# A planned transformer layer on one core: where a quarter of x is reloaded, and how the planner counts GpSimd DMAs

## The chip, the cores and the metric

The kernel runs on one core of a Trainium2 chip, as one launch. The metric is device time in microseconds (us), the median of three runs of the same program. A further execution was recorded by the hardware profiler; its own time stands in the table below. A core has five engines with an instruction queue each: TensorE (PE in the profile, PEld for its weight loads), VectorE (DVE), ScalarE (ACT), GpSimd (POOL) and SyncE (SP, which here only issues DMAs). Each queue is worked off in order. POOL issues DMAs as well, those that add to what lies in the destination.

## The reference

One layer of a hybrid encoder for 1024 tokens of width 1024, float32. Cut to what matters here:

```python
proj = x @ w_in                       # q, k, v and a forget gate of 8 heads; a second branch; two gates
log_fa = log_sigmoid(f_a + b_f);  F = cumsum(log_fa)
s = q_t . k_s / 8 + F[t] - F[s],  causal;   y_a = softmax(s) @ v        # forgetting attention, 8 heads of 64
y_b = rms_norm(hgrn2(q_b, f_b, i_b)) * norm_g * sigmoid(g_b)             # gated linear recurrence, 4 heads of 128
merged = sigmoid(gate_a) * (y_a @ w_pa) + sigmoid(gate_b) * (y_b @ w_pb)
x = layer_norm(ALPHA * x + merged @ w_o)
x = layer_norm(ALPHA * x + swiglu_ffn(x))
```

## The kernel before, in words

**Precision.** A float32 product is made of three PE matmuls: each operand is split into a rounded high part and the rest (`split`: an ACT copy and a DVE subtraction), and `mm3` multiplies high by high, high by low and low by high.

**Strassen.** Large products run as seven products of quarters instead of eight. x, transposed and split, is held in quarters A11, A12, A21 and A22. `quarter(i, m)` is half i of the channels at half m of the tokens: A21 is `quarter(0, 1)` and A22 is `quarter(1, 1)`; a21 and a22 are the same quarters before the split. Sums of quarters (S1 to S4 in the text below) are made by DVE. S1 takes the place of A21 (`vops["p5"] = A21`, L667), so that A21 must be made again from a21 before its plain use.

**Stages, in the order of the program text.** (1) The products for v and for a value of the second branch, and the forget gates; the sums of the latter go to DRAM as nf_d. (2) `qk_all` makes q and k of the 8 heads in four calls of `qk_strassen`, for pairs of heads in the order 0, 1, 2, 3 (`QORDER`, L36); results go to DRAM as qk_d through `put`. (3) `attention` for four pairs of heads. (4) The second branch, head by head: `hgrn_project` (matmuls bps) and `hgrn`. (5) Gates (ge, gs), the branch projections (pps), the output projection (o), layer norm, the feed-forward part (fa, fb, fc, p), layer norm. Matmuls of (4) and (5) that depend only on x, bps and ge, are filler for PE while (3) and (4) wait on other engines. bps reads both token halves of x, so it needs A21 whole; ge of `gate_part` needs only the first halves.

**box1** (L575) is one 128 x 4 x 1024 tile. First its rows 0 and 1 hold a21 and its rows 2 and 3 hold a22. While the sums are made (L679 to L688) a21 is overwritten by s3 = A11 - a21, which is split for product p7 and stored to DRAM (`sum_d[1]`, L687); then a21 is loaded into the same rows again (L688). In the last call of `qk_strassen`, behind product p5, `split4(A21, a21)` (L764) makes A21 from it.

Later box1 holds the masks of the attention. Head h uses rows r and r+1 with r = 2 for even h and 0 for odd h (L807). Row r gets the head's forget sums, row r+1 the causal constant, both by SP; then POOL issues a DMA that adds the forget sums to row r+1:

```python
sync.dma_start(box1[:, r, :], nf_d[h].partition_broadcast(P))
sync.dma_start(box1[:, r + 1, :], a["causal"])
pool.dma_start(box1[:, r + 1, :], nf_d[h].partition_broadcast(P), accum_op=ALU.add)
```

Each of the three moves 512 KB. A score block s of PSUM is added to its mask by a DVE instruction that also takes the running minimum (`p<-s,box` and `p_w<-s,box` in the profile); ACT exponentiates, POOL scales the rows by the sums' reciprocals (`p<-p,sums`), PE transposes (pt), ACT and DVE split the transposed block (th, tl), and PE multiplies by v (pv). q2, k2 and kl of a head are loaded from qk_d (`qk_load`, L785), k2 and kl into tiles of the tag kb.

**Tiles and slots.** A tile is taken by tag, and each tag has a fixed number of slots (`BUFS`, L399). Tag tt has four slots of 128 x 512; in the stages around the change it holds t2, u2 and the high parts of `put` in each `qk_strassen`, and th and tl in the attention. Tag kb has four; in this stage two are held by the operand S4 of product p3 (L697) and two by the weights of pair 1.

**The order is planned.** The kernel's text doesn't set the order of the instructions. A class `Plan` (L63) records every call with its dependencies. `schedule` (L182) plays the calls through a model with a cost for each: at each step it takes the call that can start first, and by rank among equals. `improve` (L352) then does this `ROUNDS` = 36 more times: each time `latest` computes the latest start of every call from the last result, with a slack that is drawn at random from the seventh round on, and uses it as rank. The order with the earliest modelled end is emitted. In the model SP's transfers run one after the other at 300 bytes per ns (`dma_free`, the time when they are through). A POOL DMA occupies POOL for `SOFT` = 950 ns and lands `LANDS` + bytes / `RATE` = 1050 ns + 524288 / 190 ns later; of POOL's DMAs at most `RING` = 3 are under way, and each lands at least its transfer after the one before.

Nearly every instruction is issued from one line, L384, so the rows of the profile are told apart by the names of their tiles.

Of the kernel before, what the change touches and what calls it, by code (L numbers as in the profile page):

```python
# [62 lines left out]
class Plan:  # L63
# [118 lines left out]
    def schedule(self, slack, wait):  # L182
        calls = self.calls
        tiles = {k: list(v) for k, v in self.tiles.items()}
        users = [[] for _ in calls]
        left = []
        for i, c in enumerate(calls):
            left.append(len(c[4]))
            for m in c[4]:
                users[m].append(i)  # L190
        ready = [0.0] * len(calls)
        self.took, self.after, self.users = [0.0] * len(calls), [], users
        gave = {}
        avail = {q: [] for q in self.queues}
        free = {q: 600.0 for q in self.queues}
        dma_free = 0.0
        ring = [0.0] * RING
        fifo, slots = {}, {}
        for name, i in sorted(self.first.items(), key=lambda kv: (self.turn[kv[1]], kv[1])):
            tag, bufs = self.tiles[name][:2]  # L200
            fifo.setdefault(tag, []).append(name)
            slots.setdefault(tag, [(0.0, "")] * bufs)
        head = dict.fromkeys(fifo, 0)
        for tag in fifo:
            fifo[tag].reverse()
        held = set()
        table = None
        order = {q: [] for q in self.queues}
        for i, c in enumerate(calls):
            if not left[i]:  # L210
                avail[c[0].name].append(i)
        done = 0
        self.times = [0.0] * len(calls)
        while done < len(calls):
            best = None
            for q, av in avail.items():
                for i in av:
                    t = max(free[q], ready[i])
                    ok = True
                    need = {}  # L220
                    for name in calls[i][6]:
                        if name in held:
                            continue
                        tag = self.tiles[name][0]
                        k = need.get(tag, 0)
                        if tag not in LOOSE and name not in self.loose and (len(fifo[tag]) <= k or fifo[tag][-1 - k] != name):
                            ok = False
                            break
                        if len(slots[tag]) <= k:
                            ok = False  # L230
                            break
                        t = max(t, sorted(slots[tag])[k][0] + 60)
                        need[tag] = k + 1
                    if not ok:
                        continue
                    if self.lands[i]:
                        t = max(t, ring[-RING])
                    if q == "ACT":
                        kind = self.kind(calls[i])
                        if kind is not None and kind != table:  # L240
                            t += wait
                    if best is None or (t, self.rank[i]) < best[:2]:
                        best = (t, self.rank[i], i, q)
            if best is None:
                raise RuntimeError("no call can be placed")
            t, _, i, q = best
            c = calls[i]
            avail[q].remove(i)
            d = c[7] * (1 if q in ("PE", "SP") else MARGIN)
            if q == "DVE" and c[8]:  # L250

                d += 0.7 * min(d, max(0.0, free["POOL"] - t))
            if q == "SP":
                start = max(t + 100, dma_free)
                dma_free = start + d
                free[q] = t + 500
                fin = dma_free
            else:
                if q == "ACT":
                    kind = self.kind(c)  # L260
                    if kind is not None and kind != table:
                        table = kind
                        t -= wait
                        d += 1283
                free[q] = t + d
                fin = t + d + self.lands[i]
                if self.lands[i]:
                    fin = max(fin, ring[-1] + self.lands[i] - self.LANDS)
                    ring.append(fin)
            self.times[i] = t  # L270
            self.took[i] = d
            order[q].append((t, i))
            for name in c[6]:
                if name in held:
                    continue
                held.add(name)
                tag = self.tiles[name][0]
                fifo[tag].remove(name)
                s = slots[tag]
                old = min(s)  # L280
                s.remove(old)
                self.after.append((old[1], i))
            for name in c[5]:
                rec = tiles.get(name)
                if rec:
                    rec[2] -= 1
                    rec[3] = max(rec[3], fin + self.LAT[q])
                    if rec[2] == 0:
                        slots[rec[0]].append((rec[3], name))
            for u in users[i]:  # L290
                uq = calls[u][0].name
                lat = self.OWN[q] if uq == q else self.LAT[q]
                if uq == "PE" and q != "PE":
                    lat += slack
                elif uq == "POOL" and q != "POOL":
                    lat += 27
                ready[u] = max(ready[u], fin + lat)
                left[u] -= 1
                if not left[u]:
                    avail[uq].append(u)  # L300
            done += 1
        self.end = max(dma_free + self.LAT["SP"], *free.values())
        return sorted((t, i) for v in order.values() for t, i in v)
# [48 lines left out]
    def improve(self, slack, wait):  # L352


        self.turn = list(range(len(self.calls)))
        best = self.schedule(slack, wait), self.end, self.times
        sound = self.turn, self.rank
        vary = np.random.default_rng(3)
        for n in range(ROUNDS):
            self.rank = self.latest(slack if n < 6 else slack * vary.uniform(0, 3))  # L360
            self.turn = self.rank
            try:
                order = self.schedule(slack, wait)
            except RuntimeError:
                self.turn, self.rank = sound
                order = self.schedule(slack, wait)
            sound = self.turn, self.rank
            if self.end < best[1]:
                best = order, self.end, self.times
        order, self.end, self.times = best  # L370
        return order
# [16 lines left out]
def trunk(ctx: ExitStack, tc, a: dict, out: bass.AP):  # L388
    nc = tc.nc
    plan = Plan(tc)  # L390
    sync, act, dve, pool, pe = (plan.queue(n, e) for n, e in (
        ("SP", nc.sync), ("ACT", nc.scalar), ("DVE", nc.vector), ("POOL", nc.gpsimd), ("PE", nc.tensor)))
# [23 lines left out]
    def half(tag, name, dt=F32):  # L416
        return take(tag, [NB], name, dt)
# [14 lines left out]
    def hs(i):  # L432
        return slice(i * NB, (i + 1) * NB)
# [7 lines left out]
    def split(hi, lo, src):  # L441
        act.copy(hi, src)
        dve.tensor_sub(lo, src, f(hi))
# [64 lines left out]
    def split4(op, raw):  # L508
        for c in range(4):
            split(op[0][c], op[1][c], raw[c])  # L510

    A11, A12, A21, A22 = quarter(0, 0), quarter(1, 0), quarter(0, 1), quarter(1, 1)
# [37 lines left out]
    for k, b, A, p, o in ((0, b11, A11, "p1", vx), (1, b21, A12, "p2", vy)):  # L550
        T = stationary4("v" + p)
        raw = rows(b)
# [24 lines left out]
    a21, a22 = ([box1[:, 2 * i + c // 2, hs(c % 2)] for c in range(4)] for i in range(2))  # L577
# [101 lines left out]
    for c in range(4):  # L679
        s3 = a21[c]  # L680
        dve.tensor_sub(s3, f(A11[0][c]), s3)
        dve.tensor_add(s3, s3, f(A11[1][c]))
        dve.tensor_sub(a22[c], a22[c], s3)
        split(vops["p6"][0][c], vops["p6"][1][c], a22[c])
        split(vops["p7"][0][c], vops["p7"][1][c], s3)
        sync.dma_start(sum_d[0, c], a22[c])
        sync.dma_start(sum_d[1, c], s3)  # L687
        sync.dma_start(s3, a["xT"][c][:, hs(1)])  # L688
    product("p6", T2, vx, True)
    for t in range(4):  # L690
        dve.tensor_add(vbm[:, t, :], vx[t], p1v[t])
# [39 lines left out]
    def qk_strassen(p, wtags, btags, last=False):  # L731
# [29 lines left out]
        dve.tensor_sub(b12, b12, b11)  # L761
        mul("p5", b12, oc, True)
        if last:
            split4(A21, a21)  # L764
        t2 = take("tt", [4, P], f"wqk{p}_t2")
        dve.tensor_sub(t2, b22, b12)
        mul("p2", b21, ob, True)
# [111 lines left out]
    raw = half("gt", "once_r")  # L879
# [371 lines left out]
    for i, src in enumerate((ya_d, yb_d)):  # L1251
        yh, yl = [], []
        for c in range(4):
            if i == 0:
                raw, rest = (take(f"wr{a_}", [S], f"yr{a_}{c}") for a_ in range(2))
# [547 lines left out]
```

## Time and profile before

| | us |
|---|---|
| median of 3 runs | 1436.33 (1436.11 to 1436.84) |
| the profiled execution, its own time | 1436.61 |
| span of its instructions | 1434.8 |
| mean granted TensorE clock | 0.996 |
| PE busy | 1419.1 (99% of the span) |
| DVE busy | 1104.8 (77%) |
| ACT busy | 657.0 (46%) |
| POOL busy | 90.9 (6%) |

The span begins at 0 with the first instruction, and all times in the rows are counted from there. A row of a timeline has start, duration, engine, line, operation, output<-inputs, shapes and a count; in square brackets stands the idle time of the engine before it and who ended it. In the view of waits a row says who waited for whom, the total in us, how often, and the longest. In the table of windows each row is a stretch of time with, for PE, PEld, DVE, ACT and POOL, the busy time and in brackets the number of instructions, then the granted clock of PE as a share of full speed, the busy share of the 16 DMA engines, and GB/s. Rows of DMA issues end with the median us from issue to landing. Matmul ends are modelled and overlap, so the rate of matmuls is read from the distance of their starts.

### The profile page before, as it was taken

Reading aid. Unit: us, or ns where it says so; the run is one execution under the profiler, and the core shown is the slowest. Engines: PE = TensorE matmul, PEld = TensorE weight load, DVE = VectorE, ACT = ScalarE, POOL = GpSimd, SP = SyncE. Lnnn points to the kernel's source line nnn. Section 1 sums busy time; section 2 is a strip of 40 time slices with the busy share of each in tenths; the row PEclk is TensorE's granted clock in tenths of the full one; section 3 lists DMA queues with packets and bytes.
Section 4 is the critical chain, followed back from the end, with each engine's and each line's share of the span. In section 5 each row is a group of like instructions: output and inputs, shape, how many; then the busy total and the mean of one; then the engine's idle time right before and its main releaser. Section 6 shows DMA issues by size and latency. Waiting matters only on the chain.

```text
span 1434.8 us, 18979 instructions
## 1 busy us (share of the span) xinstructions
PE 1419.1 (99%) x6722; PEld 1180.1 (82%) x6722; DVE 1104.8 (77%) x1912; ACT 657.0 (46%) x1164; POOL 90.9 (6%) x108
## 2 busy tenths in 40 slices
PE   9999989999999999999999999999999999999997
PEld 7788878888888888888888888888888888888886
DVE  7995868899888978546757997666766776789597
ACT  5534668986778632244511543333333334444330
POOL 0000233420001000000001000000000000000001
PEclk9999999999999999999999999999999999999999
DMA  7456999811112677457500233333333325878632
GB/s 269 168 181 234 290 270 280 236 60 45 45 59 75 217 229 231 151 199 271 176 1 20 84 103 119 101 104 110 110 111 110 100 93 200 326 257 271 215 130 88
DMA packets 92158, 227.39 MB, mean 158 GB/s; under 512 B 10512, under 2 KB 11792, under 8 KB 92064
## 3 DMA queue, kind: packets, MB, share of 16 engines
q1 hardware_dynamic: 90912, 221.99, 47.1%
q0 software_dynamic: 1152, 4.19, 1.5%
q8 instruction: 53, 0.87, 0.3%
q14 instruction: 41, 0.34, 0.1%
HBM read 167.62 MB, written 58.52 MB: 158 GB/s over the span
## 4 chain that ended last, share of the span: by engine, by line
PE 95%; DVE 3%; DMA 1%; ACT 1%; issue 0%; POOL 0%; SPq 0%; DVEq 0%; POOLq 0%
PE p L384 15%; PE fb L384 11%; PE bps L384 9%; PE gs L384 8%; PE fc L384 8%; PE fa L384 8%; PE o L384 6%; PE pps L384 6%; PE vx L384 4%; PE qk_s L384 2%; PE s L384 2%; PE vy L384 2%; PE pv L384 2%; PE ge L384 2%; PE qk_h L384 2%; PE pt L384 2%
## 5 line engine op out<-in xcount | busy, mean ns | idle before, releaser
L384 PE MATMUL p<-dp 128*128 128x512 f32 (+1 forms) x957 | 210.0, 382 | 0.0
L384 PEld LDWEIGHTS p<-dp 128*128 128x128 f32 x957 | 175.3, 188 | 34.8
L384 PE MATMUL fc<-xs,Tp 128*128 128x512 f32 x528 | 127.3, 389 | 0.8 <-ACT Tp L384 0.8
L384 PE MATMUL fb<-xs,Tp 128*128 128x512 f32 x528 | 127.2, 389 | 0.0
L384 PEld LDWEIGHTS fc<-xs,Tp 128*128 128x128 f32 x528 | 99.1, 188 | 21.8 <-ACT Tp L384 1.2
L384 PEld LDWEIGHTS fb<-xs,Tp 128*128 128x128 f32 x528 | 99.1, 188 | 20.5
L384 PE MATMUL fa<-x,Tp 128*128 128x512 f32 x480 | 115.6, 389 | 0.0
L384 ACT CAST Tp<-t 128x512 fp32r<-128x512 f32 x88 | 54.1, 620 | 118.5 <-PE fc L384 64.8
L384 DVE TENSOR_TENSOR Tp<-t,Tp 128x512 fp32r<-128x512 f32 x88 | 60.7, 691 | 61.2 <-ACT Tp L384 60.6
L384 PEld LDWEIGHTS fa<-x,Tp 128*128 128x128 f32 x480 | 90.1, 188 | 18.7
L384 PE MATMUL bps<-xh,wb_h 128*128 128x512 f32 x192 | 76.9, 401 | 0.1
L384 PE MATMUL bps<-xl,wb_h 128*128 128x512 f32 x192 | 76.6, 400 | 0.0
L384 PE MATMUL bps<-xh,wb_l 128*128 128x512 f32 x192 | 76.6, 402 | 0.0
L384 POOL TENSOR_TENSOR norm<-norm,few 128x1 f32<-128x1 f32 x16 | 15.4, 963 | 910.7 <-DVE norm L384 910.7
L384 ACT CAST dp<-dap 128x1024 fp32r<-128x1024 f32 (+1 forms) x42 | 41.1, 979 | 54.2 <-PE p L384 32.3
L384 DVE TENSOR_TENSOR dp<-dap,dp 128x1024 fp32r<-128x1024 f32 (+1 forms) x42 | 47.5, 1132 | 22.2 <-ACT dp L384 22.2
L384 DVE TENSOR_TENSOR tl<-pt,th 128x512 fp32r<-128x512 f32 (+1 forms) x96 | 51.3, 551 | 9.5 <-ACT th L384 5.3
L384 PE MATMUL fb<-x,Tp 128*128 128x512 f32 x240 | 57.6, 389 | 0.0
L384 ACT CAST Tp<-wg_r 128x512 fp32r<-128x512 f32 x40 | 24.9, 623 | 62.0 <-PE fb L384 30.0
L384 PEld LDWEIGHTS fb<-x,Tp 128*128 128x128 f32 x240 | 45.0, 188 | 9.4
L384 ACT CAST th<-pt 128x512 fp32r<-128x512 f32 (+1 forms) x96 | 45.2, 478 | 15.5 <-PE pt L384 8.9
L384 DVE TENSOR_TENSOR u<-fb,p 128x512 f32<-128x512 f32 x40 | 27.7, 692 | 29.4 <-PE fb L384 29.4
(705 smaller groups left out, 3456.5 us busy)
## 6 DMA issues: line engine op xcount, KB each, us to landing
dbp<-in_w_fo SPq DMA_DIRECT2D x45, 512.0 KB, 4.7
dap<-a_d SPq DMA_DIRECT2D x35, 512.0 KB, 4.6
wg_r<-in_w_ff SPq DMA_DIRECT2D x22, 512.0 KB, 3.7
wu_r<-in_w_ff SPq DMA_DIRECT2D x22, 512.0 KB, 3.7
a_d<-ar SPq DMA_DIRECT2D x42, 256.0 KB, 2.7
a_d<-as SPq DMA_DIRECT2D x33, 256.0 KB, 2.3
qk_d<-qk SPq DMA_DIRECT2D x32, 256.0 KB, 4.4
wg_r<-in_w_g SPq DMA_DIRECT2D x16, 512.0 KB, 4.6
```

Source lines behind the costliest of these rows:

```text
L384: getattr(q.engine, method)(*args, **kw)
```

## The change

Three edits. (1) The reload of a21 into box1 behind the stores of the sums is gone. Instead, in the last `qk_strassen`, each of its four parts is loaded into a tile of tag tt, and split into A21 from there. The same bytes are loaded, and the same splits are made. (2) In `schedule` the landing of a POOL DMA is put off by the time for which SP's transfers are still under way when it is issued, and half of its transfer time is charged to `dma_free`, so that later SP transfers are put off as well. (3) The random generator of `improve` starts from seed 1 instead of 3.

```diff
@@ Plan.schedule
                 free[q] = t + d
                 fin = t + d + self.lands[i]
                 if self.lands[i]:
+                    fin += max(0.0, dma_free - t - d)
+                    dma_free = max(dma_free, t + d) + 0.5 * (self.lands[i] - self.LANDS)
                     fin = max(fin, ring[-1] + self.lands[i] - self.LANDS)
                     ring.append(fin)
@@ Plan.improve
-        vary = np.random.default_rng(3)
+        vary = np.random.default_rng(1)
@@ trunk, the sums of the quarters
         sync.dma_start(sum_d[0, c], a22[c])
         sync.dma_start(sum_d[1, c], s3)
-        sync.dma_start(s3, a["xT"][c][:, hs(1)])
@@ qk_strassen
         mul("p5", b12, oc, True)
         if last:
-            split4(A21, a21)
+            for c in range(4):
+                raw = half("tt", f"a21_{c}")
+                sync.dma_start(raw, a["xT"][c][:, hs(1)])
+                split(A21[0][c], A21[1][c], raw)
         t2 = take("tt", [4, P], f"wqk{p}_t2")
```

## The prediction

> **What bounds the kernel now.** First the page, for the room that TensorE (PE) leaves at all.
>
> ```profile
> span 1434.8 us, 18979 instructions
> ...
> PE 1419.1 (99%) x6722; PEld 1180.1 (82%) x6722; DVE 1104.8 (77%) x1912; ACT 657.0 (46%) x1164; POOL 90.9 (6%) x108
> ```
>
> PE is idle for 1434.8 - 1419.1 = 15.7 us. No other order can win more than that and what a slow clock costs. Next the view of waits, of PE over the whole span; it names all of PE's waits:
>
> ```profile
> PE s L384 <- DVE soft L384: 5.1, 1, 5.1
> PE vy L384 <- DVE few L384: 1.2, 1, 1.2
> PE fc L384 <- ACT Tp L384: 0.8, 1, 0.8
> PE s L384 <- DMA kl<-qk_d: 0.6, 1, 0.6
> PE pt L384 <- DVE tl L384: 0.2, 1, 0.2
> ```
>
> They sum to 7.9 us. The other 7.8 us is nearly all tail: in the chain of waits the last run of matmuls ends at 1384.96 + 42.38 = 1427.34, 7.5 us before the span does.
>
> ```profile
> 1384.96 42.38 PE p L384 x218
> ```
>
> The change edits nothing there. So one wait is worth looking at, the 5.1 us before a score matmul (s). PE's timeline around it:
>
> ```profile
> 178.54 0.65 PE L384 MATMUL s<-kl,q 128*128 128x128 f32 x3 [0.65 <-DMA kl<-qk_d]
> ...
> 180.28 0.39 PE L384 MATMUL bps<-xh,wb_l 128*128 128x512 f32 x1
> 180.51 0.39 PE L384 MATMUL bps<-xh,wb_h 128*128 128x512 f32 x1
> 186.01 0.69 PE L384 MATMUL s<-k,q 128*128 128x384 f32 x1 [5.12 <-DVE soft L384]
> ...
> 188.10 0.63 PE L384 MATMUL bps<-xh,wb_l 128*128 128x512 f32 x1
> 188.53 0.63 PE L384 MATMUL pv<-th,vhl 128*128 128x512 f32 x1
> ```
>
> A 512-column matmul follows the last one after 0.23 us ahead of the gap and after 0.43 us behind it. The windows of 2 us show why; the column behind POOL's is the granted clock:
>
> ```profile
> 184.00:186.00 2.00, 0.00 (x0) 0.00 (x0) 0.34 (x3) 0.01 (x1) 0.06 (x1) 0.50 1.02 258
> 186.00:188.00 2.00, 1.99 (x5) 1.79 (x6) 1.49 (x8) 2.00 (x7) 0.81 (x1) 0.50 1.04 372
> 188.00:190.00 2.00, 2.00 (x6) 1.52 (x6) 1.21 (x4) 0.39 (x2) 0.00 (x0) 0.50 1.02 408
> 190.00:192.00 2.00, 2.00 (x12) 1.72 (x11) 1.53 (x4) 1.97 (x3) 1.39 (x3) 0.80 1.07 261
> ```
>
> All engines stand still, and the clock is halved inside the gap. From 186 on it costs 2 x 0.50 + 2 x 0.50 + 2 x 0.20 = 2.4 us more. Only the DMA engines (the share behind the clock) are full. What did DVE wait for? DVE's, POOL's and SP's timelines:
>
> ```profile
> 165.23 0.69 DVE L384 TENSOR_TENSOR xl<-box,xh 128x512 fp32r<-128x512 f32 x1
> ...
> 185.66 0.29 DVE L384 CUSTOM_DVE_ANT_0 p<-s,box 128x128 f32<-128x128 f32 x1 [8.56 <-DMA box<-nf_d]
> ...
> 199.58 0.29 DVE L384 CUSTOM_DVE_ANT_0 p<-s,box 128x128 f32<-128x128 f32 x1 [0.36 <-PE pt L384]
> ```
>
> ```profile
> 98.28 1.06 POOL L384 DMA_DIRECT2D box<-nf_d  x1 [97.85 <-DVE vbm L384]
> ...
> 170.07 4.65 POOL L384 TENSOR_SCALAR p<-p,sums 128x640 f32<-128x640 f32 x4 [4.89 <-DVE sums L384]
> 174.67 0.89 POOL L384 DMA_DIRECT2D box<-nf_d  x1
> 185.94 0.87 POOL L384 DMA_DIRECT2D box<-nf_d  x1 [10.38 <-DMA box<-in_causal]
> ```
>
> ```profile
> 56.75 2.18 SPq L384 DMA_DIRECT2D box<-in_xT  x4
> ...
> 162.37 0.32 SPq L384 DMA_DIRECT2D box<-nf_d  x1
> ...
> 166.43 0.54 SPq L384 DMA_DIRECT2D box<-in_causal  x1
> ...
> 168.21 1.33 SPq L384 DMA_DIRECT2D kl<-qk_d  x2
> ...
> 173.92 0.33 SPq L384 DMA_DIRECT2D box<-in_causal  x1
> ```
>
> Head 0's mask is issued by POOL at 98.28, long before its use. Head 1's lies in box1 rows 0 and 1, which hold a21, reloaded at 56.75 and not read out before the last xl<-box at 165.23 + 0.69 = 165.9. So its causal part is issued at 166.43, and POOL, which first ends four scalings, adds to it at 174.67. That lands 10.83 us later by the chain of waits, at 185.5, and DVE goes on at 185.66:
>
> ```profile
> 174.67 10.83 DMA box<-nf_d
> ```
>
> **The change part by part.** *Removed:* the four reloads of 56.75. They cost SP 2.18 us; no PE wait in the list above is near 57 us, so their going wins nothing. Rows 0 and 1 are then free from about 57 us on, since the reload too had to wait until they were read out; nf_d, which the mask needs, exists by 98.28, when head 0's POOL DMA reads it. *Moved:* head 1's two SP loads, of 0.32 + 0.54 us, and its POOL DMA of 0.89 us go from 162-175 to about 98-115. SP passes them ahead of the weights of pairs 2 and 3 and of everything at 120-162, POOL ahead of all its scalings. That is 1.5 MB. Is there room?
>
> ```profile
> 104.00:110.00 6.00, 6.00 (x28) 4.97 (x27) 2.98 (x7) 2.51 (x5) 0.00 (x0) 1.00 1.00 332
> 110.00:116.00 6.00, 6.00 (x28) 4.98 (x27) 3.16 (x5) 1.57 (x3) 0.00 (x0) 1.00 0.19 73
> ...
> 146.00:152.00 6.00, 6.00 (x29) 4.95 (x28) 5.18 (x9) 3.23 (x7) 0.00 (x0) 1.00 0.77 301
> ```
>
> At 332 GB/s 1.5 MB are 4.7 us, and 110-116 alone has 0.81 x 6 = 4.9 us of idle DMA. The mask is there some 50 us before head 1 needs it, and costs nothing. *Added:* four 256 KB loads of a21 (again about 2.2 us of SP) in the last strassen, 5 to 25 us ahead of splits that end at 165.9: an estimate from the landings below, 140-158. At 301 GB/s 1 MB is 3.5 us of full DMA; 146-152 has 0.23 x 6 = 1.4 us free, so some 2 us of backlog may be left at 158. Nothing waits for PE there yet. Against it stand the 1.5 MB that no longer go out at 162-185: at the 258 GB/s of the gap 6 us less ahead of all that follows. ACT and DVE split the same four halves, from another tile, at the same price. *A new wait:* each raw tile needs one of the four tt slots, which the puts of q and k, t2, u2 and the attention's th and tl turn over. SP issues in order, so a raw load that waits for a slot holds back the qk_d stores and the q, k and kl loads of heads 0 and 1, and PE waits for those (0.65 us at 178.54). Below: nothing (PE has no wait there to win back), when the planner puts the loads where slots are free. Above: one landing of a qk_d store (10.4 us, next fence) for each round. I take nothing, and price the upper end as a rival.
>
> So **what goes** is 5.12 + 2.4 = 7.5 us. **What is late next?** First kl, then head 2's mask; the DMA issues of 164-172, 172-176 and 176-186, with median us to landing at the end:
>
> ```profile
> qk_d<-qk SPq DMA_DIRECT2D x2, 256.0 KB, 10.4
> ...
> kl<-qk_d SPq DMA_DIRECT2D x2, 256.0 KB, 9.4
> ...
> box<-in_causal SPq DMA_DIRECT2D x1, 512.0 KB, 11.7
> ...
> box<-nf_d POOLq DMA_DIRECT2D x1, 512.0 KB, 8.4
> ```
>
> Head 1's kl needs a kb slot and so can't be issued before 168.21; it lands at about 178.5. DVE could then start at about 178.9, not 185.66; PE has work until 180.9. The 5.12 us go, the 0.65 us I keep. Head 2's causal part (173.92 + 11.7 = 185.6) and POOL's add (185.94 + 8.4 = 194.3) are used at 199.58, which comes at about 192 without the gap. Unmoved, the mask would be 2.2 us late; with 6 us less ahead of it, it is in time by some 4 us.
>
> **The planner's two edits** reorder everything. The new model delays a GpSimd DMA by SP's backlog and charges SP half its transfer. By the code the old one let it land 1.05 + 2.76 = 3.8 us after issue; the rows say 10.83 and 8.4, so later masks are planned nearer the truth. Seed 1 draws other slacks. Neither adds an instruction. The size of what an order leaves in small waits is that of the short ones above, 0.2 to 1.2 us; I take no change, and 2 us either way.
>
> **Sum**, against the profiled execution (1436.61 us, 1.8 outside its span): 1436.6 - 7.5 = 1429.1. The median of the three runs is 0.3 lower, which gives 1428.8. I predict 1429.0. Removing all five PE waits would be 1436.3 - 7.9 - 2.4 = 1426.0, the floor.
>
> **The rivals.** (A) *Head 2's mask, or another, takes the gap's place.* DMA is full behind the gap (1.02 to 1.07 in 184-192, above), and the gap gave later transfers 7.5 us of lead. Unmoved, head 2's costs 2.2 us: 1431.2; with a halved clock behind it 2.2 + 2.4: 1433.6; two such, 1438, which is its far end. For it: masks land 8 to 12 us after issue. Against it: the bytes taken out, and a plan that knows of them. [...]
>
> (B) *Nothing comes of it:* the planner, free to choose, still places head 1's mask or something else that scores need (q and k come late through the same full DMA) so that the 5.1 us stay: 1435 to 1438.
>
> (C) *Slower: the tt slots.* Two raw loads wait a round each, SP stands still behind them, and A21 is whole late. Before, it is whole at 165.9 and the filler matmuls (bps) that read it start at 171.93:
>
> ```profile
> 171.93 0.39 PE L384 MATMUL bps<-xh,wb_h 128*128 128x512 f32 x1
> ```
>
> That is 6.0 us of cover. One round (10.4) and a landing (5.4, the median of box<-in_xT among the DMA issues, below) make 15.8 us; 9.8 of it is PE idle, and 2.4 of clock make 12.2. Less the 7.5 won: 1436.3 + 4.7 = 1441. It decides from 6.0 + 5.1 = 11.1 us of lateness on, and counts as slower from 14. For it: four more tiles of some 7 us each in four slots while two strassens overlap. Against it: the planner counts slots, and puts of pairs 2 and 3 are not urgent.
>
> ```profile
> box<-in_xT SPq DMA_DIRECT2D x12, 256.0 KB, 5.4
> ```
>
> **How the numbers follow.** The forecast (1426 to 1431.2) has 0.54; A 0.20, B 0.08, C 0.18. This kernel's measurement tells 0.2%, 2.9 us, from no change: faster is below 1433.5, slower above 1439.2. Faster: the forecast and 0.12 of A, 0.66. Same: 0.08 of A and B, 0.16. Slower: C, 0.18. The range reaches from 0.5 above the floor to the end of B, 1426.5 to 1438.0, and leaves out C and a little at the floor. The forecast's own range is 1426.5 to 1431.2.
>
> **What would show it.** POOL issues two adds to box near 98-105, the next not before 175. DVE's 8.56 us wait for box and PE's 5.12 us are gone, and the clock is 1.00 in all windows from 160 to 200. box<-in_xT appears near 140-158, into other tiles. A shows as POOL or DVE waiting for box with PE idle near 185-200; C as an SP wait ahead of the raw loads and PE idle at 160-175. A new PE wait over 3 us elsewhere would mean that the reordering, not the mask, decides.

## The result, and the profile after

| | us |
|---|---|
| kernel after, median of 6 runs | 1428.11 (1427.25 to 1428.72) |
| kernel before, median of 6 runs beside it | 1436.22 (1435.34 to 1437.18) |
| ratio after / before | 0.9943, 95% interval 0.9930 to 0.9956 |
| profiled execution of after, its own time | 1427.78 (before 1436.61) |

The change makes the kernel 8.1 us faster; the profiled executions differ by 8.8 us. First the page of after, its span and busy times:

```profile
span 1425.8 us, 18971 instructions
...
PE 1415.6 (99%) x6722; PEld 1178.1 (83%) x6722; DVE 1104.2 (77%) x1912; ACT 659.1 (46%) x1166; POOL 89.2 (6%) x108
```

The span is 9.0 us shorter. PE's idle time is now 1425.8 - 1415.6 = 10.2 us instead of 15.7: 5.5 us less. The other 3.5 us are busy time that went; 2.4 of them are the halved clock behind the old gap, and 1.1 I can't tie to a place. Next the whole list of PE's waits in after:

```profile
PE vy L386 <- DVE few L386: 1.2, 1, 1.2
PE fc L386 <- ACT Tp L386: 0.8, 1, 0.8
PE s L386 <- DVE soft L386: 0.3, 1, 0.3
PE pt L386 <- DVE tl L386: 0.3, 1, 0.3
```

They sum to 2.6 us against 7.9. The 5.1 us before a score matmul are gone, and so are the 0.6 us for kl. The windows of 2 us where before had stood still, columns as above:

```profile
184.00:186.00 2.00, 1.73 (x9) 1.17 (x8) 1.11 (x5) 1.99 (x6) 0.77 (x2) 1.00 1.03 411
186.00:188.00 2.00, 2.00 (x12) 1.59 (x12) 1.84 (x10) 2.00 (x6) 2.00 (x4) 1.00 1.02 400
188.00:190.00 2.00, 2.00 (x11) 1.73 (x10) 0.87 (x2) 2.00 (x4) 0.46 (x2) 1.00 1.10 352
```

PE works, the clock is 1.00, and the DMA engines are as full as they were. Three timelines of after show the moved work: POOL, then SP, then DVE.

```profile
99.41 1.98 POOL L386 DMA_DIRECT2D box<-nf_d  x2 [98.98 <-DVE wqk_t L386]
...
187.25 0.85 POOL L386 DMA_DIRECT2D box<-nf_d  x1
```

```profile
58.13 0.36 SPq L386 DMA_DIRECT2D box<-in_causal  x1
...
75.78 0.33 SPq L386 DMA_DIRECT2D box<-in_causal  x1
...
100.15 0.86 SPq L386 DMA_DIRECT2D box<-nf_d  x2
...
152.62 0.39 SPq L386 DMA_DIRECT2D a<-in_xT  x1
...
170.06 0.34 SPq L386 DMA_DIRECT2D a<-in_xT  x1
...
177.59 0.34 SPq L386 DMA_DIRECT2D box<-in_causal  x1
```

```profile
174.35 0.29 DVE L386 CUSTOM_DVE_ANT_0 p<-s,box 128x128 f32<-128x128 f32 x1 [0.35 <-POOL p L386]
...
176.57 1.22 DVE L386 TENSOR_TENSOR xl<-a,xh 128x512 fp32r<-128x512 f32 x1 [1.10 <-ACT xh L386]
...
199.45 0.29 DVE L386 CUSTOM_DVE_ANT_0 p<-s,box 128x128 f32<-128x128 f32 x1
```

The masks of heads 0 and 1 are both begun at 58 to 76 and both added to at 99.41. Head 1's is first read at 174.35 instead of 185.66, and nobody waited for it. In the same stretch a21 comes in raw, the fourth part issued as late as 170.06 and split until 176.57 + 1.22 = 177.8, after the first bps of PE's timeline:

```profile
170.12 0.39 PE L386 MATMUL bps<-xh,wb_h 128*128 128x512 f32 x1
```

Head 2's mask, issued from 177.59 on and added to at 187.25, is read at 199.45.

### The profile page after: what moved, and what is told of

It reads as the page before. It is cut to its first block, busy times and chain, and to the rows that moved or that the text cites. A ratio compares the mean times of both kernels' runs of the same rounds, so it can differ in the third digit from the quotient of the medians.

```text
span 1425.8 us, 18971 instructions
## 1 busy us (share of the span) xinstructions
PE 1415.6 (99%) x6722; PEld 1178.1 (83%) x6722; DVE 1104.2 (77%) x1912; ACT 659.1 (46%) x1166; POOL 89.2 (6%) x108
## 4 chain that ended last, share of the span: by engine, by line
PE 77%; DVE 2%; ACT 0%; issue 0%; DVEq 0%
PE p L386 15%; PE fb L386 11%; PE gs L386 8%; PE fc L386 8%; PE fa L386 8%; PE bps L386 7%; PE o L386 6%; PE pps L386 6%; PE ge L386 2%; PE lp L386 2%; PE op L386 1%; PE pv L386 1%; PE pt L386 1%; DVE xs L386 0%; PE x1t L386 0%; PE up L386 0%
```

## The experiments

**The theories.** The first is that of the prediction: head 1's mask came late, everything waited for it, and after is faster because that mask is there early. Its rival: each of the three edits makes the planner draw another order of the whole kernel, and what decides is which transfer that order leaves late in the stretch where DMA is full. The two part where the mask alone is moved in an order held fixed, and where the edits are taken singly or with other seeds. Each kernel computes the whole layer. The kernel before ran beside them on the same chips, with medians of 1435.86, 1436.92 and 1436.13 us for the first four, the next four and the last four runs. Those of before moved by up to 1.1 us from one set to the next, so that differences of 1 us between runs of different sets tell nothing. Letters in the expectations name theories, M the first of the two above; rivals A to C are those of the prediction. Below, "the reload" is the new place of a21's reload, "the cost" the new cost of a POOL DMA.

**1. Head 1's mask back where it was, in after's order.** One line in the function that emits the calls gives three DMAs other places in the queues and leaves every other instruction in its order:

```diff
-        order = self.improve(slack, wait)
+        at = dict(zip(range(self.mask[1], self.mask[1] + 3), (161900.0, 165000.0, 174020.0)))
+        order = sorted((at.get(i, t), i) for t, i in self.improve(slack, wait))
```

(`mask[h]` is the number of the first of the three mask calls of head h, noted where they are recorded; times in ns.)

> The changed kernel with its own order held instruction by instruction on all engines; only head 1's three mask DMAs are moved back to about where the kernel before had them (its two SP loads among the k loads near 162-166, the POOL add just ahead of the first read, near 175). Theory M (the time is lost where a mask lands after its planned first read): add issued near 175, landing 8 to 11 us later, DVE waits 9 to 12 us from 174.4 on, PE idles 5 to 8 us with the clock halved behind it: 1435 to 1440. Rival R (the new order and seed did it, the mask's place is worth little because the new order has filler there): at most 1431. Rival D (what helped is the 1.5 MB taken out of the full DMA stretch): some of the loss without a DVE wait for box, 1430 to 1433.

Measured: 1439.54 us (1439.01 to 1443.32, 5 runs), ratio to before 1.0034 [1.0020, 1.0049]. POOL's timeline, DVE's, then PE's waits and its windows:

```profile
175.46 0.88 POOL L386 DMA_DIRECT2D box<-nf_d  x1
```

```profile
185.41 0.29 DVE L386 CUSTOM_DVE_ANT_0 p<-s,box 128x128 f32<-128x128 f32 x1 [11.05 <-DMA box<-nf_d]
```

```profile
PE pt L386 <- DVE tl L386: 8.6, 2, 8.4
```

```profile
182.00:184.00 2.00, 0.00 (x0) 0.00 (x0) 0.00 (x0) 0.00 (x0) 0.00 (x0) 0.71 1.00 260
184.00:186.00 2.00, 0.00 (x0) 0.00 (x0) 0.59 (x3) 0.00 (x0) 0.00 (x0) 0.50 1.12 299
186.00:188.00 2.00, 1.64 (x6) 1.54 (x7) 1.38 (x4) 1.36 (x4) 1.41 (x1) 0.50 0.99 328
```

The gap is back, with the halved clock, and DVE stands 11.05 us for the mask. Three DMAs moved, and all of the gain is lost and 3 us more: 11.4 us over after. The early mask is needed for after's time. Rival D, by which only the bytes taken out of the full stretch had helped, expected no such wait for box; those bytes came back as well, so what they cost by themselves is not told apart. In that order PE reaches the mask sooner than before did (DVE's wait begins at 174.36 instead of 177.10), so that the gap is 8.4 us and not 5.1.

**2. The same three; the second is planned 2.5 us and the third, the add, 6 us earlier than in 1** (161900, 162500, 168000).

> As late_add_held, but the three mask DMAs are moved back less: SP loads near 162, POOL add between its scalings near 168 to 172. [...] R: 1428 to 1429, no PE wait.

Measured: 1437.19 us (1435.25 to 1440.42, 10 runs), 1.0011 [1.0002, 1.0021]. POOL's timeline and PE's waits:

```profile
172.27 0.91 POOL L386 DMA_DIRECT2D box<-nf_d  x1 [5.58 <-DMA box<-in_causal]
```

```profile
PE pt L386 <- DVE tl L386: 6.2, 2, 5.9
```

POOL waited for the causal part, so the add went out only 3.2 us earlier than in 1, and the gap shrank by 2.5. It was meant to leave a gap of a few us and so to show the clock behind a short one; it left 5.9, and the clock fell as in 1, to 0.50 in 180 to 186. What it does show is the slope: 3.2 us of the add's start are 2.5 us of gap and 2.4 us of time. The intervals of the two ratios touch, so it rests on the rows more than on the times.

**3. The new cost alone** (before with the cost, seed 3).

```diff
                 if self.lands[i]:
+                    fin += max(0.0, dma_free - t - d)
+                    dma_free = max(dma_free, t + d) + 0.5 * (self.lands[i] - self.LANDS)
```

> The kernel before with the planner's new cost of POOL DMAs alone (a21 still reloaded early into box1, seed 3). Here the planner puts head 1's first read some 15 us after the POOL add (by its own times 193 and 178), where the kernel before had 5. M: the mask is late but nobody waits for it, PE has other matmuls there: 1430.5 to 1433.5, no DVE wait for box over 2 us. Rival E (only the early mask, so only the reload, removes the gap): 1435 to 1438, the PE wait of about 5 us still there.

Measured: 1441.20 us (1439.12 to 1447.02, 5 runs), 1.0044 [1.0026, 1.0063]. DVE's timeline and PE's waits:

```profile
191.03 0.69 DVE L386 TENSOR_TENSOR tl<-pt,th 128x512 fp32r<-128x512 f32 x1 [10.39 <-DMA qk_d<-qk]
```

```profile
PE pt L386 <- DVE tl L386: 9.8, 2, 9.2
```

A miss. DVE waits for no mask here, though head 1's add goes out only at 178.25, and yet it is the slowest of all. DVE wants a tt slot for a tl, and the slot is held by a part of q or k that `put` is still storing. Such stores take 11.3 us to land in this stretch (the median of qk_d<-qk among the DMA issues of 164 to 186). That nobody waits for the mask is not enough.

**4. The reload alone** (before with the reload, seed 3).

```diff
-        sync.dma_start(s3, a["xT"][c][:, hs(1)])
...
-            split4(A21, a21)
+            for c in range(4):
+                raw = half("tt", f"a21_{c}")
+                sync.dma_start(raw, a["xT"][c][:, hs(1)])
+                split(A21[0][c], A21[1][c], raw)
```

> The kernel before with the new place of the reload alone (old cost of POOL DMAs, seed 3). Head 1's mask is early. Head 2's add is planned at 185 and its first read at 190, with a landing 3.8 us after issue; measured landings are 8 to 11 us. M: the gap at head 1 goes and a shorter one opens at head 2: DVE waits 3 to 6 us, PE idles 0 to 3 us: 1430 to 1434. Rival E (the reload is the whole gain): 1428 to 1429.5, no new wait for box.

Measured: 1435.65 us (1431.93 to 1437.41, 10 runs), 0.9996 [0.9986, 1.0005]: no gain. POOL's timeline, DVE's, PE's waits, and the windows:

```profile
185.03 0.89 POOL L384 DMA_DIRECT2D box<-nf_d  x1
```

```profile
195.06 0.29 DVE L384 CUSTOM_DVE_ANT_0 p<-s,box 128x128 f32<-128x128 f32 x1 [5.31 <-DMA box<-nf_d]
```

```profile
PE pv L384 <- DVE tl L384: 4.1, 1, 4.1
```

```profile
194.00:196.00 2.00, 0.39 (x2) 0.39 (x3) 0.57 (x4) 0.00 (x0) 0.28 (x1) 0.92 1.05 246
196.00:198.00 2.00, 2.00 (x8) 1.71 (x7) 1.57 (x6) 1.63 (x5) 0.84 (x1) 0.50 1.02 266
198.00:200.00 2.00, 2.00 (x10) 1.53 (x9) 0.82 (x4) 1.19 (x4) 0.00 (x0) 0.73 1.04 195
```

This is rival A of the prediction in full: head 1's mask is early, so head 2's is asked for at 195.06 - 5.31 = 189.75, 9.8 us sooner than before's 199.58, and it is the one that is late. The gap is 4.1 us, and the halved clock behind it costs 0.16 + 1.00 + 0.54 = 1.7 us more: 5.8 of the 7.5 us won are given back at the next mask, and the rest goes into small waits.

**5. Reload and cost together, seed 3 kept.**

> Both mechanisms of the change, seed 3 as before: the reload's new place and the new cost of POOL DMAs. Theory M2 (each of the two edits alone leaves a wait: the reload alone one at head 2's mask, the cost alone one elsewhere in the full DMA stretch; together they leave none, and the seed is incidental): 1427.5 to 1431, no PE wait over 2 us between 140 and 300. Rival S (the seed was picked for the chip; other seeds leave gaps as before): 1433 to 1441.

Measured: 1437.82 us (1436.12 to 1440.18, 10 runs), 1.0010 [1.0001, 1.0019]. ACT's timeline and PE's:

```profile
187.06 0.58 ACT L386 CAST th<-pt 128x512 fp32r<-128x512 f32 x1 [4.62 <-DMA qk_d<-qk]
```

```profile
188.42 1.12 PE L386 MATMUL pt<-ident,p 128*128 128x128 f32 x4 [4.18 <-DVE tl L386]
```

Both masks are in time here, and the place of the late transfer is taken by a store that holds a tt slot. So with seed 3 the two real edits do not give the gain either; after differs from this kernel by one digit, the seed, and by 9.7 us.

**6, 7, 8. The other three combinations**: the cost with seed 1, the reload with seed 1, and seed 1 alone.

```diff
-        vary = np.random.default_rng(3)
+        vary = np.random.default_rng(1)
```

> The change without the reload's new place: new cost of POOL DMAs, seed 1, head 1's mask still in rows that are free only near 166. M2: its planned first read is some 14 us after the add, so no wait for box, but three mask DMAs (1.5 MB) stay in the full stretch 160-190 and a store or load there lands later than planned: a PE wait of 2 to 10 us as with the cost alone: 1434 to 1442. Rival P (honest costs are enough, the model_only loss was a matter of its seed): 1429 to 1434.

> The change without the new cost of POOL DMAs: reload in its new place, seed 1. Head 2's add is planned at 184 and its first read at 190, as in reload_only. M2: a wait for box at head 2 of 3 to 6 us on DVE, 2 to 5 us on PE: 1431 to 1436. Rival S (the seed is what counts): about 1428.

> The kernel before with seed 1 alone. Head 1's add is planned at 173 and its first read at 177. M2: DVE waits 5 to 9 us for box at head 1, as before: 1434 to 1438. Rival S: about 1428 to 1431.

Measured: 1434.47 us (1432.95 to 1435.70, 10 runs), 0.9983 [0.9974, 0.9993]; 1439.78 (1436.11 to 1441.81, 10 runs), 1.0021 [1.0011, 1.0030]; 1437.47 (1434.14 to 1439.59, 10 runs), 1.0003 [0.9992, 1.0014]. PE's waits of the first of them, the cost with seed 1:

```profile
PE pt L386 <- DVE tl L386: 2.5, 4, 1.2
PE gs L386 <- DVE gu L386: 1.4, 2, 1.0
```

the two longest of the reload with seed 1:

```profile
PE pt L384 <- POOL p_w L384: 2.6, 1, 2.6
PE qk_h L384 <- ACT qk_p L384: 1.9, 1, 1.9
```

and of seed 1 alone, DVE's and PE's:

```profile
DVE p L384 <- DMA box<-nf_d: 4.5, 1, 4.5
```

```profile
PE s L384 <- DVE soft L384: 4.0, 1, 4.0
```

Seed 1 alone waits for head 1's mask as seed 3 did. The first loses its time in many waits of 1 us. Of the second's two longest waits, the one of 2.6 us, near 308, is behind POOL's scalings, with neither mask nor store in it, and a halved clock follows. The one of 1.9 us, near 116, is behind a store again: ACT, which makes qk_p, had just stood 5.2 us for a store of v (v_d<-v). All its PE waits come to 10.4 us against 2.6 in after, and the halved clock adds 1.7: 9.5 of the 11.3 us between the two profiled executions. All eight combinations:

| | seed 3 | seed 1 |
|---|---|---|
| neither | 1436.2 (before) | 1437.5 |
| the reload | 1435.7 | 1439.8 |
| the cost | 1441.2 | 1434.5 |
| reload and cost | 1437.8 | 1428.1 (after) |

No edit has a price of its own. The reload moves the time by -0.5, +2.3, -3.4 or -6.4 us, depending on what else is set, the cost by between +5.0 and -11.7, the seed by between +4.1 and -9.7.

**9. Head 2's mask a little earlier, in the order of 4.** Its causal part goes ahead of one kl load on SP, its add ahead of one scaling on POOL; all else is held.

```diff
-        order = self.improve(slack, wait)
+        at = {self.mask[2] + 1: 174600.0, self.mask[2] + 2: 183500.0}
+        order = sorted((at.get(i, t), i) for t, i in self.improve(slack, wait))
```

> reload_only with its own order held; only head 2's causal load moves up by one kl load in SP's queue and its POOL add up by one scaling (512 wide) in POOL's, as early as head 0's last read of that row allows. Theory W (reload_only lost its gain to head 2's mask, and only to that): the add is issued some 2 us earlier, DVE's wait for box falls from 5.3 to about 3 us, PE's gap from 4.1 to 1 to 2.5 us, and the halved clock may go: 1430.5 to 1434 against 1435.65. Theory S (the loss is spread over the new order, one wait replaces the next): 1435 to 1436.

Measured: 1434.44 us (1431.99 to 1437.86, 11 runs), 0.9988 [0.9979, 0.9997], against 0.9996 [0.9986, 1.0005] of 4. POOL's timeline and PE's waits:

```profile
183.82 0.91 POOL L384 DMA_DIRECT2D box<-nf_d  x1 [2.21 <-DVE sums L384]
```

```profile
PE pv L384 <- DVE tl L384: 2.8, 1, 2.8
```

The add could go only 1.2 us earlier, since POOL still stood behind scalings that waited for sums. The gap fell from 4.1 to 2.8, by 1.3: in this order head 2's mask does end the wait, us for us. The median fell by 1.2, but the two intervals overlap, so the runs alone would not show it.

**10, 11, 12. Further seeds:** all edits with seeds 4 and 10, and the kernel before with seed 6.

> The changed kernel with seed 4 in place of 1. Theory S (in the stretch where the DMA engines are full, each order has some transfer that lands later than planned; the seed decides whether someone waits for it): anywhere from 1428 to 1441, with a PE wait of 2 to 9 us between 170 and 200 when it is above 1432; no wait for head 1's mask in any case. Theory M2 (both edits together are enough): 1428 to 1431.

> The changed kernel with seed 10, whose order has nearly the modelled end of seed 1's (0.4 us later by the planner's own model). S: 1428 to 1441, the modelled end tells little. M2: 1428 to 1430.

> The kernel before with seed 6 in place of 3; head 1's mask free only near 166, its add planned at 173, its first read at 176. W and S alike: DVE waits 5 to 10 us for head 1's mask, as before and with seed 1: 1434 to 1440. If it came out below 1431, the reload's place would not be needed at all.

Measured: 1433.14 us (1430.85 to 1435.12, 8 runs), 0.9977 [0.9966, 0.9987]; 1431.67 (1431.06 to 1433.19, 6 runs), 0.9971 [0.9959, 0.9984]; 1440.07 (1438.66 to 1441.44, 8 runs), 1.0025 [1.0015, 1.0036]. PE's longest wait in each of the three:

```profile
PE pt L386 <- DVE tl L386: 2.8, 3, 2.1
```

```profile
PE pt L386 <- DVE tl L386: 1.7, 1, 1.7
```

```profile
PE s L384 <- DVE soft L384: 6.2, 1, 6.2
```

In the first two, DVE waited with a tl for a store (qk_d<-qk) that held a tt slot, for 4.0 us (in two waits) and 2.3 us. In the third it waited for head 1's mask, for 6.6 us at the longest.

**What follows.** Sort the orders by what is in them. The old text, with seeds 3, 1 and 6, gives 1436.2, 1437.5 and 1440.1: mean 1437.9, and in each PE stands still for 4.0 to 6.2 us over head 1's mask. The new text, with seeds 1, 3, 4 and 10, gives 1428.1, 1437.8, 1433.1 and 1431.7: mean 1432.7, and none waits for that mask; three of the four wait for a store in its stead. So the change is worth about 5 us over these few orders. The spread is 3.9 us within the old text and 9.7 within the new, and of the 35 ways to pick three of these seven times, 3 pick times as slow as the old text's or slower: that the new text is faster in the mean is likely, not shown. The reload alone and the cost alone, with two seeds each, have means of 1437.7 and 1437.8, no better than the old text. After is the best order of those tried, by 3.6 us over the next. Why seed 1's order leaves no slot behind a late store stays open: the stores' median landing does not tell it (7.3 us in after, 6.6 in 5, 8.2 and 9.3 with seeds 10 and 4).

## Why the prediction came right, and which step of it failed

- *The gap and the clock behind it, 7.5 us:* right, and shown by 1. Together with the 0.65 us for kl, which I kept and which went, that is 8.1 to 8.2 us, the measured difference of the medians. The sum was short by that one term.
- *Head 1's mask DMAs at 98 to 115 cost nothing:* right. The adds went out at 99.41 and landed 10.9 us later, some 60 us ahead of their use.
- *Head 2's mask in time by some 4 us:* right for after. With 8.9 us, the median landing of the adds in 177 to 202, it is there at 196.2 and read at 199.45, 3.3 us to spare. But it is no property of the change: in 4 it was 5.3 us late, and rival A happened there.
- *Nothing for the tt slots, with 6.0 us of cover and a bound of 11.1 us (rival C):* the outcome was right and the reason wrong. A21 was whole at 177.8, 11.9 us later than before's 165.9, beyond the bound, and PE did not wait: bps begins 7.7 us before A21 is whole, so its first matmuls don't read all of it. I had taken the start of the first bps for the moment at which A21 is needed. The slots did cost, but in other orders and elsewhere: not a raw load waiting for a store, but DVE and ACT waiting for a th or tl behind one (3, 5, 10, 11).
- *The planner's two edits: "I take no change, and 2 us either way":* **this step failed.** I sized it by the short waits that were left in one order, 0.2 to 1.2 us. The same text with four seeds spans 1428.1 to 1437.8 us, and the cost with seed 3 alone makes 1441.2. The forecast holds only because after's order is the one in which nothing follows the gap. That is luck of the seed: nothing in the prediction says why seed 1 should draw it. By its own steps run 5, with the same two edits of substance, should have been as fast, and it was 9.7 us slower. (The 3.8 us that it gives for the old model's landing begin where POOL is through; counted from the start of the issue, as the rows count, they are 4.8.)
- *"A new PE wait over 3 us elsewhere would mean that the reordering, not the mask, decides":* after has none; 3 and 5 have one of 9.2 and of 4.2 us. Both theories hold a part: the mask had to go early, and the order had to leave nothing else late.
- *Rival A's two prices for 2.2 us of wait, 1431.2 with the clock left alone and 1433.6 with it halved:* no row of before tells which of them holds, and the runs show both kinds. The gap of 1.74 us in run 11 was followed by 1.7 us of lost clock, so that it cost 3.4 us; one of 1.92 us in run 7 lost no clock.

## What to carry to other kernels

Where the DMA engines are full (a share of about 1.0 from 160 to 200 here), a late transfer that is moved away makes the next one due sooner (head 2's mask by 9.8 us in 4): look up every transfer and every slot held by a store in that stretch, and count the gain only down to the next of them. In a planned kernel an edit and the order that is drawn for it can't be told apart by one run; run the edit with several seeds, and test its mechanism with the order held and only the suspected instructions moved. An engine's first use of a stage is not the first use of the tile that you worry about: find the row that reads the tile.

## What the runs showed of the hardware

**Behind a PE gap of 1.74 us the clock was halved, and only after PE was back at work; behind one of 1.92 us it was not.** The gap of 1.74 us is that of seed 10 (run 11). PE's timeline, then windows of 1 us:

```profile
186.16 0.44 PE L386 MATMUL pt<-ident,p 128*128 128x128 f32 x2 [1.74 <-DVE tl L386]
```

```profile
186.00:187.00 1.00, 0.84 (x6) 0.67 (x6) 1.00 (x6) 0.00 (x0) 0.34 (x1) 1.00 1.05 424
187.00:188.00 1.00, 1.00 (x5) 0.91 (x5) 1.00 (x5) 0.58 (x1) 0.00 (x0) 0.69 0.99 391
188.00:189.00 1.00, 1.00 (x4) 0.90 (x4) 0.88 (x4) 1.00 (x4) 0.01 (x1) 0.50 1.08 420
189.00:190.00 1.00, 1.00 (x4) 0.74 (x3) 0.00 (x0) 1.00 (x3) 1.00 (x2) 0.50 1.12 326
190.00:191.00 1.00, 1.00 (x6) 0.87 (x5) 0.17 (x1) 0.98 (x4) 1.00 (x2) 0.61 1.07 240
```

PE resumes at 186.16 at full clock. The clock falls at 188 - 2 x 0.31 = 187.4 and is back at 191 - 2 x 0.11 = 190.8: 3.4 us at half speed, in which PE is busy, so 1.7 us lost on top of the 1.74. Read in the same way, the halved stretch behind the gap lasts from 3.4 us in run 4 to about 10 us in run 3. Gaps of 1.74, 2.11, 2.63 and 2.79 us were followed by the lower clock; one of 1.92 us (run 7, near 116), one of 1.54 us (run 1, near 174) and those of after, 1.2 us and less, were not.

So in these runs the length of a gap near 2 us did not tell whether the clock fell: it cost 1.7 us more in run 11 and nothing more in run 7. What parts the two is not shown here.

**In the full stretch the landing of the same kind of transfer moves from order to order, and size alone doesn't tell it.** Two groups of the DMA issues of run 3 from 164 to 186, with the median us to landing at the end:

```profile
qk_d<-qk SPq DMA_DIRECT2D x4, 256.0 KB, 11.3
...
box<-nf_d SPq DMA_DIRECT2D x1, 512.0 KB, 11.0
```

Here twice the bytes land no later. Over the whole of before the 32 stores of this kind land in 4.4 us at the median, in this stretch in 10.2. In the same stretch of after they took 7.3 us and with seed 10 (run 11) 8.2, while a 512 KB load of the forget sums took 8.6 and 8.8 there: the larger one was later in these orders. In run 5 the stores took 6.6 us. So the same kind of transfer's landing moves by 4.7 us from one order to another.
